# Two-layer decoder trunk: the second layer's residual and softmax sums turned by VectorE and placed through DRAM by GpSimd, and the first two blocks of a tail run in turns

## The chip, the cores and the metric

One core of a Trainium2 chip runs the whole program. The metric is device time in microseconds (us) of one execution, as the median of several runs. The engines are called as in the profile: PE is TensorE's matmul, PEld its weight load, DVE is VectorE, ACT is ScalarE, POOL is GpSimd, and SP is the engine that issues the transfers (DMAs) of the kernel before.

## The reference

The input has 1024 tokens of width 1024. Two layers follow each other; everything is float32.

```python
# layer 0: gated linear attention, layer 1: sparse attention with an indexer
y = gla_mixer(x, ...)   # then   y = dsa_mixer(x, ...)
x = layer_norm(ALPHA * x + y, ln_g[i], ln_b[i])                 # ALPHA = 4 ** 0.25
x = x + (p[i] @ ple_w[i]) * jax.nn.sigmoid(x @ ple_gate_w[i])   # the tail of a layer
# dsa_mixer, for each block of 128 queries:
score = sum over 8 index heads of relu(qi @ ki) * wi            # causal
idx = top 256 keys of each query
probs = softmax(q @ k[idx] * 128 ** -0.5)                       # 16 heads of 128, one k and v for all
o = probs @ v[idx]
return (o * silu(z)) @ w_out
```

## The kernel before

Products are made in three passes: a factor is split into a high part and the rest (`whi`, `wlo` for weights; `xh`, `xl` for activations), and high x high, high x low and low x high are added in one PSUM bank. So most of PE's work is 128x128 weights against 128x512 values, three for each 128 of depth; a block of 128 outputs over depth 1024 (`fm_block`) is 24 of them.

The tokens are done in two halves of 512. Layer 0 is done for both halves, then layer 1's index scores and top-k selection are set up, then layer 1 is done for half 0 and for half 1. Within layer 1 a half is a row of *slots*, one for each of the 16 heads: in a slot PE runs two or three blocks of projections (queries `dq`, gates `dz`, outputs `do`) with the attention of one head threaded between them. A head's scores of four query tiles (`A(t)`, into `P`) are exponentiated by ACT into `sq`, turned by DVE in squares of 32 (L1559), stored to DRAM (`sqd`), and loaded back turned (`PT`); ACT and DVE split them (`ph`, L1597 and L1599) and PE multiplies by the values (`o`). The store of a head must be done before ACT may write the next head's exponentials to `sq`.

The order of each engine is written by the program itself: `Flow` keeps a clock of PE's planned time, `fl.at(t, f)` and `after(dt, f)` put a step where that clock passes t, and every engine then takes its instructions in the order in which they were written. A wait of one instruction holds all that stand behind it on that engine. SP issues all transfers of the kernel before, on one queue.

Three places matter here.

- **The residual of layer 1.** x lies in DRAM (`x2s`) with features in rows; it is needed with tokens in rows (`y`), scaled by ALPHA. In each of the first four slots of a half, `residual` loads two tiles of 128 features x 512 tokens (`xst`, L1495), PE turns each with four transposes into a PSUM bank (`by_token`, L1500), and ACT copies it to `y` (L1501). The output products (`do`) add to `y`, and their first needs all eight.
- **The softmax sums.** For each head, `inverse` takes the reciprocal of the sums (`sm`, L1605), `turn` transposes them on PE into a PSUM bank (L1611), ACT copies them (L1616), SP stores them as a `row` (L1617), and `to_all` loads them into all partitions (`inv`, L1625), for DVE to multiply into the gate (L1647).
- **The tail.** After the normalization, PE transposes y (`xpose`), ACT and DVE make the split tiles of x (`gx` and others), and eight gate blocks follow one after the other; the first walks over the eight tiles of x as they come.

In layer 0, `squares_out` and `squares_in` already bring a result to the other orientation in the way that the change uses: DVE turns squares (L731), SP stores four quarters to DRAM (`od`, L750) and loads them back (`uf`, L756).

Of the kernel before, what the change touches and what calls it, by code (L numbers as in the profile page):

```python
# [20 lines left out]
D = 1024  # L21
L = 1024
NH = 2
HT = 512
# [253 lines left out]
def trunk_kernel(ctx, tc, x_tok, x_T, p_T, pos, freq, g_q, g_k, g_v, g_z, g_a, g_a2, g_ba, g_gn, g_o,  # L278
# [178 lines left out]

    def narrow(w, n, t):
# [170 lines left out]
    def core_steps(u):  # L629
# [175 lines left out]
    def accumulate(parts, U, y, ch, rs=None, norm=None, ahead=1):  # L805
# [5 lines left out]
        for t, b in order:  # L811
# [11 lines left out]
            ys = y[:, t, ch * 512:ch * 512 + 512]  # L823
            if rs is not None:
                dve.scalar_tensor_tensor(ys, ps, rs[:, t:t + 1], ys, op0=OP.mult, op1=OP.add)
            else:
                dve.tensor_add(ys, ps, ys)  # L827
# [26 lines left out]
    def norm_steps(y, np_, eps, on_act=()):  # L854
# [6 lines left out]
        def norm(t, ch):  # L861
# [7 lines left out]
            dve.bn_stats(st8[:, t, ch], y[:, t, ch * 512:ch * 512 + 512])  # L869
# [5 lines left out]
            def apply():  # L875
                if t in on_act:
                    act.activation(y[:, t], y[:, t], AF.Identity, scale=rstd[:, t:t + 1], bias=mv[:, t, 1:2])
                else:
                    dve.tensor_scalar(y[:, t], y[:, t], mv[:, t, 0:1], rstd[:, t:t + 1],
                                      op0=OP.subtract, op1=OP.mult)  # L880
# [24 lines left out]
    def tail(layer, Pt, y, y_done, final, tp, xps, x_alloc, tmp, ple=(), first=None, shared=False, split_last=False):  # L905
# [10 lines left out]
        def xpose(k):  # L916
            fl.need(lambda: all(y_done))
            ps = xps()
            for t in range(4):
                fl.transpose(ps[:, t * 128:t * 128 + 128], y[:, t, k * 128:k * 128 + 128], ident)  # L920
# [20 lines left out]
        for b in range(NK):  # L941
            def ev(ps, ts=slice(0, HT), b=b):
# [3 lines left out]
                def gated():  # L946
# [3 lines left out]
                      (1.5, lambda: final(b, x1, ts) if cut else final(b, x1)))  # L950
            cut = split_last and b == NK - 1
            yield from fm_block(("t", layer, b), X, ev, *([(slice(0, 256), slice(256, HT))] if cut else []))
# [50 lines left out]
    def small_head(half, X, f32t, alloc, qalloc, tmp, spsum, kih, kil, res):  # L1003
# [30 lines left out]
        yield from fm_block(("ki",), X, ev_ki)  # L1034
        for b in range(4):
            def ev_qi(ps, b=b):
# [11 lines left out]
            yield from fm_block(("qi", b), X, ev_qi)  # L1048

    def small_kv(half, X, f32t, alloc, tmp, spsum, kh, kl, vh, vl, res):  # L1050
# [14 lines left out]
        def ev_v(ps):  # L1065
# [14 lines left out]
            chain((0, lambda: act.activation(vf, ps, AF.Copy, scale=0.5)), (1.2, turn))  # L1080
# [144 lines left out]
    def start_half(half):  # L1225
# [15 lines left out]
        def feed():  # L1241
            if half == 0:
                load(0, 1)
                W.loads(W.ns + 1)
                load(1, 1)
                W.loads(W.ns + 2)
                for k in range(2, NK, 2):
                    load(k, 2)
# [28 lines left out]
    for half in range(NH):  # L1277
        hs = slice(half * HT, half * HT + HT)
        if half == 0:
# [8 lines left out]
            feed_by(feeder, 0.0, 0.0)  # L1288
# [5 lines left out]
        y = X.y  # L1294

        def load_y(y=y, half=half):
# [50 lines left out]
        norm, y_done = norm_steps(y, lp, EPS / ALPHA ** 2)  # L1347
# [141 lines left out]
    def residual(st, y, half, ks, start, end):  # L1489

        tiles = {}

        def load(k):
# [399 lines left out]
```

## Time and profile before

| | |
|---|---|
| runs of the kernel before | 1946.26 us median of 3 (1946.18 to 1946.48) |
| the profiled execution | 1945.97 us, of which the span from its first to its last instruction is 1944.2 us |
| PE busy | 1924.8 us, 99% of the span |
| DVE, ACT, POOL busy | 1481.8, 1014.5 and 55.2 us |
| DMA | 480.50 MB, mean 247 GB/s, all but some instruction loads on SP's queue |

A row of the profile names line, engine, operation, the tile written and those read, partitions x elements, and then busy time, the mean of one, and the idle time before it with what ended most of it. In a timeline the columns are start, length, engine, line and operation. The recorded length of a matmul is longer than the time after which the next one starts: matmuls overlap, and what a matmul costs PE is the distance from its start to the next start. In a table of windows DMA share is the mean busy share of 16 DMA engines, which can come out a little over 1.

### The profile page before, as it was taken

How to read it: one execution, taken by the hardware profiler on the slowest of the kernel's cores; microseconds unless marked ns; L12 is line 12 of the kernel's file. 1: busy time of each engine (PE TensorE's matmuls, PEld its weight loads, DVE VectorE, ACT ScalarE, POOL GpSimd, SP SyncE). 2: the span in 40 equal slices, each digit the busy share in tenths (PEclk: the TensorE clock that was granted, in tenths of full speed). 3: DMA queues.
4: the chain of work that ended last, by engine and by line, in shares of the span. 5: the costliest groups of instructions: out<-in, count | busy, mean ns of one | idle time of the engine just before them, and what ended most of it. 6: DMA issues, size and time to landing. Idle time of an engine off the chain costs nothing.

```text
span 1944.2 us, 26708 instructions
## 1 busy us (share of the span) xinstructions
PE 1924.8 (99%) x8912; PEld 1596.4 (82%) x8912; DVE 1481.8 (76%) x3039; ACT 1014.5 (52%) x1930; POOL 55.2 (3%) x115
## 2 busy tenths in 40 slices
PE   9999999999999999999999999999999999999999
PEld 7888888888788888888888888888878888888877
DVE  5777666696778888888859987778797887777873
ACT  5564636445564646464635676766443554434432
POOL 0000000010000000000100000000000000000000
PEclk9999999999999999999999999999999999999999
DMA  4567776767668777677686588877867998888873
GB/s 155 201 222 229 221 226 214 227 210 268 227 196 266 226 212 233 220 226 218 207 304 222 194 308 292 276 271 259 317 221 236 365 323 300 299 297 300 294 260 144
DMA packets 195818, 480.50 MB, mean 247 GB/s; under 512 B 22496, under 2 KB 39008, under 8 KB 189536
## 3 DMA queue, kind: packets, MB, share of 16 engines
q1 hardware_dynamic: 195680, 478.79, 73.8%
q8 instruction: 70, 1.15, 0.2%
q14 instruction: 68, 0.56, 0.1%
HBM read 338.98 MB, written 139.72 MB: 246 GB/s over the span
## 4 chain that ended last, share of the span: by engine, by line
PE 88%; DVE 4%; ACT 4%; DMA 2%; issue 1%; SPq 0%; POOL 0%; ACTq 0%; DVEq 0%
PE pb L58 66%; PE o L58 8%; PE U L58 6%; PE S L58 6%; DMA wlo<-wls 1%; PE tr L58 1%; ACT x L926 1%; DVE wlo L191 0%; DVE bn L869 0%; DMA xst<-x2s 0%; DMA y<-in_x_T 0%; DVE y L827 0%; PE pb L62 0%; PE ix L58 0%; DMA row<-uf 0%
## 5 line engine op out<-in xcount | busy, mean ns | idle before, releaser
L58 PE MATMUL pb<-x,whi 128*128 128x512 f32 x2272 | 705.4, 391 | 1.1 <-DVE x L411 1.0
L58 PEld LDWEIGHTS pb<-x,whi 128*128 128x128 f32 x2272 | 418.2, 188 | 81.2 <-DVE x L411 2.2
L58 PE MATMUL pb<-x,wlo 128*128 128x512 f32 x1136 | 442.8, 390 | 0.0
L58 PE MATMUL pb<-whi,u 128*128 128x512 f32 x1024 | 339.9, 392 | 1.5 <-ACT u L419 0.8
L58 PEld LDWEIGHTS pb<-x,wlo 128*128 128x128 f32 x1136 | 213.2, 188 | 45.7 <-DVE wlo L191 0.4
L58 PEld LDWEIGHTS pb<-whi,u 128*128 128x128 f32 x1024 | 192.1, 188 | 41.4 <-ACT u L419 1.2
L58 PE MATMUL pb<-wlo,u 128*128 128x512 f32 x512 | 199.8, 390 | 0.5 <-DMA wlo<-wls 0.5
L191 DVE TENSOR_TENSOR wlo<-wst,whi 128x512 fp32r<-128x512 f32 x232 | 154.3, 684 | 37.5 <-ACT whi L189 37.4
L189 ACT ACTIVATE whi<-wst 128x512 fp32r<-128x512 f32 x232 | 136.5, 622 | 69.4 <-DMA wst<-in_g_k 23.5
L1553 ACT ACTIVATE sq<-P,mx 128x128 f32<-128x128 f32 (+7 forms) x128 | 98.9, 773 | 88.2 <-DVE mx L1546 67.5
L58 PE MATMUL S<-kT,q 128*128 128x512 f32 (+2 forms) x576 | 122.4, 342 | 0.0
L1599 ACT ACTIVATE ph<-PT 128x512 fp32r<-128x512 f32 (+2 forms) x160 | 86.6, 559 | 65.6 <-PE o L58 46.3
L58 PEld LDWEIGHTS S<-kT,q 128*128 128x128 f32 x576 | 100.8, 188 | 18.1 <-DVE mx L1546 0.7
L58 PEld LDWEIGHTS pb<-wlo,u 128*128 128x128 f32 x512 | 96.2, 188 | 19.3 <-DMA wlo<-wls 1.3
L1597 DVE TENSOR_TENSOR PT<-PT,ph 128x512 fp32r<-128x512 f32 (+2 forms) x160 | 93.3, 594 | 21.1 <-ACT ph L1599 20.7
L1180 ACT ACTIVATE tk<-sc,tki 128x768 f16<-128x768 f32 (+2 forms) x90 | 92.8, 1031 | 18.3 <-DVE tki L1189 16.1
L1559 DVE STREAM_TRANSPOSE sq<-sq 128x128 f32<-128x128 f32 (+7 forms) x128 | 97.6, 768 | 3.2 <-ACT sq L1553 3.0
L237 DVE TENSOR_TENSOR pst<-pst,phi 128x512 fp32r<-128x512 f32 x130 | 88.7, 683 | 7.5 <-ACT phi L233 7.4
L736 ACT ACTIVATE junk<-o 128x512 bf16<-128x512 f32 x32 | 19.1, 597 | 142.1 <-DVE ot L731 109.8
L58 PE MATMUL o<-ph,vT 128*128 128x512 f32 (+2 forms) x320 | 92.4, 370 | 0.2 <-ACT ph L1599 0.2
L58 PE MATMUL pb<-whi,x 128*128 128x512 f32 x256 | 85.2, 391 | 0.7 <-ACT whi L189 0.7
L58 PE MATMUL U<-whi,x 128*128 128x512 f32 x256 | 84.5, 389 | 0.0
(324 smaller groups left out, 3325.0 us busy)
## 6 DMA issues: line engine op xcount, KB each, us to landing
whi<-whs SPq DMA_DIRECT2D x128, 512.0 KB
wlo<-wls SPq DMA_DIRECT2D x128, 512.0 KB
sqd<-sq SPq DMA_DIRECT2D x192, 256.0 KB
PT<-sqd SPq DMA_DIRECT2D x48, 1024.0 KB
whs<-phi SPq DMA_DIRECT2D x130, 256.0 KB
wls<-pst SPq DMA_DIRECT2D x130, 256.0 KB
wst<-in_g_z SPq DMA_DIRECT2D x32, 512.0 KB
wst<-in_g_o SPq DMA_DIRECT2D x32, 512.0 KB
```

The lines of the kernel that those rows point to most:

```text
L58: self.pe.matmul(out, lhsT, rhs, start=start, stop=stop)
L189: self.nc.scalar.activation(hi[:, c], st[:, c], AF.Copy, scale=1.0 if gain is None else gain)
L191: self.nc.vector.tensor_sub(lo[:, c], st[:, c], hi[:, c].bitcast(F32))
L237: self.nc.vector.tensor_sub(st, st.bitcast(F32), hi.bitcast(F32))
L736: act.activation(junk, ps, AF.Square, accum_out=u["ss"][:, c:c + 1])
L926: act.activation(X1[k], ps, AF.Identity, scale=g, bias=b)
L1180: act.activation(junk()[:, :n], scs[j], AF.Sign, bias=cand[:, j:j + 1].bitcast(F32), accum_out=cnt[:, j:j + 1])
L1553: act.activation(to, rows, AF.Exp, scale=-1.0, bias=mx, accum_out=sm[:, t:t + 1])
L1559: dve.transpose(x, x)
L1597: dve.tensor_sub(lo, lo.bitcast(F32), hi.bitcast(F32))
L1599: chain((0, lambda: act.activation(hi, lo.bitcast(F32), AF.Copy)), (0.8, second))
```

## The change

- `residual` uses PE and ACT no more. POOL issues the load of a tile, DVE turns its squares of 32 into a second tile (`turn`), POOL stores that in four quarters to DRAM (`rd`, pieces of 512 bytes) and loads it back with tokens in rows (`yt`). The two tiles of a slot start 7 us apart, each turned 3.5 us of plan after its load. `y` is now a function that gives the view of a token tile: runs of 32 values with 128 between their starts. ALPHA is left out and goes into the value scale and the norm's eps instead.
- `inverse` sets a small tile to zero on POOL, DVE writes the reciprocals into it and turns it in place, and POOL stores four rows of 32 to DRAM. PE's transpose, ACT's copy and SP's store go. The step moves from 3 us before the slot's end to 8.5 us (half 0) and 12 us (half 1) after its start.
- The normalized rows of layer 1 go to eight tiles of 512 (`yn`), two for each token tile.
- `fm_two` takes two blocks and runs the first 4 (or 5) tiles of x for the one, then for the other, then the rest of each. It is used for the first two gate blocks of all four tails, and for `ki` with the first `qi` block.
- In layer 0, `s3` waits until 2.2 in place of 1.6 us after its input; at the start of the program x's tiles are split 1.3 us apart in place of at once, and the load of tiles 2 and 3 is issued ahead of the second weight.

```diff
+    def fm_two(keys, X, evacs, cut):
+        parts = [W.take(key) for key in keys]
+        banks = [pbank() for _ in keys]
+        for ks in (range(cut), range(cut, NK)):
+            for (hi, lo), ps, evac in zip(parts, banks, evacs):
+                for k in ks:
...
+                        mm(ps, l[:, at], r, i == 0, i == 3 * NK - 1)
...
-                fl.ripe(st["At", c] + 1.6)
+                fl.ripe(st["At", c] + 2.2)
...
+        yield from fm_two([("t", layer, b) for b in range(2)], X, [gate(b, False) for b in range(2)], 4)
+        for b in range(2, NK):
...
+        yield from fm_two([("ki",), ("qi", 0)], X, [ev_ki, query(0)], 5)
...
                 load(1, 1)
+                load(2, 2)
                 W.loads(W.ns + 2)
...
-            feed_by(feeder, 0.0, 0.0)
+            feed_by(feeder, 0.0, 1.3)
...
         def load(k):
-            tiles[k] = xp.tile([128, HT], F32, tag="xst", name="xst", bufs=2)
-            nc.sync.dma_start(tiles[k], x2s[k, :, half * HT:(half + 1) * HT])
-
-        def by_token(k):
-            ps = pbank()
-            for t in range(4):
-                fl.transpose(ps[:, t * 128:t * 128 + 128], tiles[k][:, t * 128:t * 128 + 128], ident)
-            act.activation(y[:, :, k * 128:k * 128 + 128], ps.rearrange("p (t c) -> p t c", c=128), AF.Copy,
-                           scale=ALPHA)
-            st["y"] = k + 1
+            pool.dma_start(tile(k), x2s[k, :, half * HT:(half + 1) * HT])
+
+        def turn(k):
+            t = tiles[k]
+            sq = tile(k)
+            dve.transpose(sq.rearrange("p (m b i) -> p b m i", m=4, b=4), t)
+            after(1.0, lambda: away(k))
+
+        def away(k):
+            rd = dp.tile([4, 32, 4, 128], F32, tag="rd", name="rd", bufs=4)
+            for a in range(4):
+                pool.dma_start(rd[:, :, a].rearrange("m r x -> r m x"),
+                               tiles[k][32 * a:32 * a + 32].rearrange("p (m x) -> p m x", m=4))
+
+            def back():
+                pool.dma_start(y[:, k], rd.rearrange("m r a x -> (m r) (a x)"))
+                st["y"] = st.get("y", 0) + 1
+            after(3.0, back)
 
         for i, k in enumerate(ks):
-            fl.at(start + 0.6 * i, lambda k=k: load(k))
-            fl.at(end - 3.6 + 1.6 * i, lambda k=k: by_token(k))
+            fl.at(start + 7.0 * i, lambda k=k: load(k))
+            fl.at(start + 3.5 + 7.0 * i, lambda k=k: turn(k))
...
-            dve.reciprocal(st["sm", h], st["sm", h])
-            after(1.5, turn)
...
-            fl.transpose(ps[0:4, 0:128], st["sm", h], ident)
+            sums = l1.tile([128, 32], F32, tag="bn", name="sums")
+            pool.memset(sums, 0.0)
+            dve.reciprocal(sums[:, 0:4], st["sm", h])
+            dve.transpose(sums, sums)
...
-                act.activation(inv, ps[0:4, 0:128], AF.Copy)
-                nc.sync.dma_start(row, inv)
+                for a in range(4):
+                    pool.dma_start(row[:, 32 * a:32 * a + 32], sums[32 * a:32 * a + 4])
...
-                fl.at(start + dur - 3.0, scale[0])
+                fl.at(start + (12.0 if half else 8.5), scale[0])
```

How the instructions stand, at three places.

**POOL, layer 1, half 0, second slot.** `sq` is the exponentials' tile, `rstd` and `mv` belong to the norm at the end of the half. Before, POOL has nothing between them:

```order
L1762 MEMSET sq 128x2048
L863 TENSOR_SCALAR rstd<-mv 128x1
L864 TENSOR_TENSOR rstd<-rstd,mhalf 128x1
L866 TENSOR_SCALAR mv<-mv,rstd 128x1
L863 TENSOR_SCALAR rstd<-mv 128x1
```

Now, from the slot's first tile on:

```order
L1527 DMA xst<-x2s 128x512
L1542 DMA y<-rd 128x512
L1538 DMA rd<-xst 32x4x128 x4
L1527 DMA xst<-x2s 128x512
L1647 MEMSET sums 128x32
L1542 DMA y<-rd 128x512
L1654 DMA row<-sums 4x32 x4
L1538 DMA rd<-xst 32x4x128 x4
```

In half 0 the memset that DVE's reciprocal waits for stands behind four stores and one load of the same slot. (In half 1 it stands one further back, behind `y<-rd` as well.)

**DVE, layer 1, half 0, third slot.** `q` is a query tile's low part, `z` the gate, `PT` the low part of the exponentials, `tk`, `tki` and `tkf` the top-k selection. Before:

```order
L1186 TENSOR_TENSOR tki<-tkf 128x4
L1187 SCALAR_TENSOR_TENSOR tki<-tki 128x4
L1189 TENSOR_SCALAR tki<-tki 128x4
L1559 STREAM_TRANSPOSE sq<-sq 128x4x3x32
L411 TENSOR_TENSOR q<-qf,q 128x512
L1559 STREAM_TRANSPOSE sq<-sq 128x16x32
L1462 SCALAR_TENSOR_TENSOR z<-z,pb 128x512
L1597 TENSOR_TENSOR PT<-PT,ph 128x4x128
L1136 TENSOR_SCALAR tk,tkf<-sc_9850,tki 128x640
L1597 TENSOR_TENSOR PT<-PT,ph 128x4x96
L1605 RECIPROCAL sm<-sm 128x4
```

After:

```order
L1532 STREAM_TRANSPOSE xst<-xst 128x4x4x32
L1163 TENSOR_SCALAR tk,tkf<-sc_9850,tki 128x640
L1600 STREAM_TRANSPOSE sq<-sq 128x4x3x32
L1213 TENSOR_TENSOR tki<-tkf 128x4
L1214 SCALAR_TENSOR_TENSOR tki<-tki 128x4
L1216 TENSOR_SCALAR tki<-tki 128x4
L411 TENSOR_TENSOR q<-qf,q 128x512
L1600 STREAM_TRANSPOSE sq<-sq 128x16x32
L1491 SCALAR_TENSOR_TENSOR z<-z,pb 128x512
L1648 RECIPROCAL sums<-sm 128x4
L1649 STREAM_TRANSPOSE sums<-sums 128x32
L1638 TENSOR_TENSOR PT<-PT,ph 128x4x128
```

The turn of the slot's first tile has come in, and the reciprocal, eight instructions after it, stands ahead of the split of `PT` in place of behind two thirds of it.

**PE, the tail of layer 1, half 0**, from the fourth tile of x in the first gate block. `gx`, `z` and `rt` are the split tiles of x in their order, z the first. Before, the second gate block begins at the last row:

```order
L58 MATMUL pb<-gx,whi 128x512 x2
L58 MATMUL pb<-gx,wlo 128x512
L58 MATMUL pb<-gx,whi 128x512 x2
L58 MATMUL pb<-gx,wlo 128x512
L58 MATMUL pb<-gx,whi 128x512 x2
L58 MATMUL pb<-gx,wlo 128x512
L58 MATMUL pb<-gx,whi 128x512 x2
L58 MATMUL pb<-gx,wlo 128x512
L58 MATMUL pb<-gx,whi 128x512 x2
L58 MATMUL pb<-gx,wlo 128x512
L58 MATMUL pb<-z,whi 128x512 x2
```

After:

```order
L58 MATMUL pb<-gx,whi 128x512 x2
L58 MATMUL pb<-gx,wlo 128x512
L58 MATMUL pb<-z,whi 128x512 x2
L58 MATMUL pb<-z,wlo 128x512
L58 MATMUL pb<-z,whi 128x512
L58 MATMUL pb<-rt,whi 128x512
L58 MATMUL pb<-z,wlo 128x512
```

The second block's first four tiles now stand between the first block's fourth and fifth tile.

More of the change, by code (lines that the diff above doesn't have):

```diff
@@ L875, in apply @@
             def apply():
[L876 to L880, printed above, removed]
+                for there, row in to(t):
+                    if t in on_act:
+                        act.activation(there, row, AF.Identity, scale=rstd[:, t:t + 1], bias=mv[:, t, 1:2])
+                    else:
+                        dve.tensor_scalar(there, row, mv[:, t, 0:1], rstd[:, t:t + 1],
+                                          op0=OP.subtract, op1=OP.mult)
                 f_done[t] = True
@@ L940, in tail, with gate, ev @@
             yield
-        for b in range(NK):
-            def ev(ps, ts=slice(0, HT), b=b):
+        def gate(b, cut):
+            def ev(ps, ts=slice(0, HT)):
                 sg = tmp()[:, ts]
@@ L950, in ev @@
                       (1.5, lambda: final(b, x1, ts) if cut else final(b, x1)))
+            return ev
+        yield from fm_two([("t", layer, b) for b in range(2)], X, [gate(b, False) for b in range(2)], 4)
+        for b in range(2, NK):
             cut = split_last and b == NK - 1
-            yield from fm_block(("t", layer, b), X, ev, *([(slice(0, 256), slice(256, HT))] if cut else []))
+            yield from fm_block(("t", layer, b), X, gate(b, cut),
+                                *([(slice(0, 256), slice(256, HT))] if cut else []))
     def rope_tables():
@@ L1032, in weights, with query, ev_qi @@
             res["w"] = wt
-        yield from fm_block(("ki",), X, ev_ki)
-        for b in range(4):
-            def ev_qi(ps, b=b):
+        def query(b):
+            def ev_qi(ps):
                 qf = f32t()
@@ L1047, in ev_qi @@
                 rope(qf, ci, si, swap_i, tmp, stack)
-            yield from fm_block(("qi", b), X, ev_qi)
+            return ev_qi
+        yield from fm_two([("ki",), ("qi", 0)], X, [ev_ki, query(0)], 5)
+        for b in range(1, 4):
+            yield from fm_block(("qi", b), X, query(b))
     def small_kv(half, X, f32t, alloc, tmp, spsum, kh, kl, vh, vl, res):
@@ L1245, in feed @@
                 load(1, 1)
+                load(2, 2)
                 W.loads(W.ns + 2)
-                for k in range(2, NK, 2):
-                    load(k, 2)
+                load(4, 2)
+                load(6, 2)
                 nc.sync.dma_start(ba, g_ba)
@@ L1293, in trunk_kernel, with y, load_y @@
             X, units, feeder, _ = nxt
-        y = X.y
-        def load_y(y=y, half=half):
+        def y(t, a, n, tile=X.y):
+            return tile[:, t, a:a + n]
+        def load_y(y=X.y, half=half):
             nc.sync.dma_start(y, x_tok[half * HT:(half + 1) * HT, :].rearrange("(t p) d -> p t d", p=128))
```

47 lines of the change are left out of this document (32 added, 15 removed).

## The prediction

> **What bounds the kernel.** I read the page first, then the groups and waits of PE, then its timeline where it stops, then a table of windows for the slots of layer 1 that hold the residual.
>
> ```profile
> span 1944.2 us, 26708 instructions
> PE 1924.8 (99%) x8912; PEld 1596.4 (82%) x8912; DVE 1481.8 (76%) x3039; ACT 1014.5 (52%) x1930; POOL 55.2 (3%) x115
> PE 88%; DVE 4%; ACT 4%; DMA 2%; issue 1%; SPq 0%; POOL 0%; ACTq 0%; DVEq 0%
> ```
>
> PE is the bound from end to end: 99% busy, and 88% of the chain that ended last. An instruction taken off PE is therefore worth its distance to the next start, as long as nothing that PE needs comes later. The profiled execution took 1945.97 us (1.8 us around the span), 0.3 under the median of 1946.26; sums below are made against 1945.97.
>
> ```profile
> 1130.00:1147.00 17.00, 16.82 (x87) 13.75 (x86) 13.82 (x38) 14.60 (x34) 0.00 (x0) 1.00 0.85 300
> 1147.00:1164.00 17.00, 16.01 (x82) 13.30 (x81) 14.16 (x40) 14.11 (x34) 0.00 (x0) 1.00 0.83 288
> 1516.00:1537.00 21.00, 21.00 (x106) 17.68 (x105) 19.24 (x41) 11.42 (x23) 0.00 (x0) 1.00 0.99 361
> 1537.00:1558.00 21.00, 21.00 (x105) 17.65 (x105) 18.08 (x38) 11.43 (x23) 0.00 (x0) 1.00 0.97 344
> 1550.00:1555.00 5.00, 5.00 (x24) 4.14 (x23) 5.00 (x8) 2.67 (x5) 0.00 (x0) 1.00 1.01 406
> ACT sq L1553 <- DMA sqd<-sq: 13.2, 4, 4.0
> ```
>
> The columns are the window, then us busy of PE, PEld, DVE, ACT and POOL, PE's clock, DMA share and GB/s. Two slots of half 0 (17 us each), two of half 1 (21 us), and a short stretch. In half 1 the DMA engines are 97 to 99% busy and DVE 86 to 92%: two resources lie close behind PE, just where the change puts more on both. The last row, from ACT's waits between 1495 and 1600 us, says that ACT already waits there for the store of the exponentials, in four slots up to 4.0 us.
>
> **What comes off PE.**
>
> ```profile
> L62 PE MATMUL pb<-ident,xst 128*128 128x128 f32 x64 | 9.6, 273 | 1.0 <-DMA xst<-x2s 1.0
> L62 PE MATMUL S<-ident,sm 128*4 128x128 f32 x32 | 8.7, 271 | 0.0
> 1113.92 0.39 PE L58 MATMUL pb<-x,wlo 128*128 128x512 f32 x1
> 1114.15 0.60 PE L62 MATMUL pb<-ident,xst 128*128 128x128 f32 x4
> 1114.50 0.72 PE L58 MATMUL o<-ph,vT 128*128 128x512 f32 x2
> 1115.06 0.39 PE L58 MATMUL o<-PT,vT 128*128 128x512 f32 x1
> ...
> 1165.80 0.34 PE L58 MATMUL o<-PT,vT 128*128 128x384 f32 x1
> 1165.97 0.27 PE L62 MATMUL S<-ident,sm 128*4 128x128 f32 x1
> 1166.00 0.71 PE L58 MATMUL pb<-x,whi 128*128 128x512 f32 x2
> 1166.54 0.40 PE L58 MATMUL pb<-x,wlo 128*128 128x512 f32 x1
> ```
>
> A matmul of 512 columns costs 0.23 us (1113.92 to 1114.15). Residual: from 1114.15 to 1115.06 stand four transposes and two matmuls, 0.91 us; without the transposes 0.46; so 0.45 for a tile, and 64/4 = 16 tiles give 7.2 us. Sums: from 1165.80 to 1166.54 is 0.74 us; a 384-column matmul (0.17, 1165.80 to 1165.97) and two of 512 make 0.63; so 0.11, and 32 of them 3.5 us. The wait for `xst` goes as well: 1.0 idle and the restart after it, say 1.2 us. All three certain as far as PE's list goes: 11.9 us.
>
> **Stops that other edits aim at.**
>
> ```profile
> 12.44 0.39 PE L58 MATMUL pb<-whi,x 128*128 128x512 f32 x1
> 13.07 0.50 PE L58 MATMUL pb<-wlo,x 128*128 128x512 f32 x1 [0.24 <-DVE wlo L191]
> ...
> 14.88 0.50 PE L58 MATMUL pb<-wlo,x 128*128 128x512 f32 x1 [0.84 <-DVE wlo L191]
> 15.21 0.63 PE L58 MATMUL pb<-whi,x 128*128 128x512 f32 x2
> 893.45 0.39 PE L58 MATMUL o<-v,Ah 128*128 128x512 f32 x1
> 894.53 0.50 PE L58 MATMUL o<-v,Al 128*128 128x512 f32 x1 [0.69 <-DVE Al L411]
> 1420.71 0.62 PE L58 MATMUL pb<-gx,whi 128*128 128x512 f32 x2
> 1426.31 0.62 PE L58 MATMUL pb<-z,whi 128*128 128x512 f32 x2
> ```
>
> Start: 12.44 to 15.21 is 2.77 us for five starts, worth 1.14; DVE was splitting x ahead of the second weight's low part. Spread 1.3 us apart, x leaves room for it; I take 1.5, bounds 0 and 1.6 (the weight's load moves behind 512 KB and could be late itself). `s3`: 0.85 lost at 894, and the added 0.6 us holds one group of three matmuls in between, 0.6; bounds 0 and 0.85. Pair of gate blocks: from the fourth tile of x (1420.71) to the next block (1426.31) are 15 starts, 3.4 us; it took 5.6, so 2.2 lost to tiles not yet split. The second block's four tiles give the fifth 12 x 0.23 = 2.7 us more time: I take 2.0, bounds 0 and 2.2. The other pairs (three tails and `ki`) show no such loss, nothing. ACT's two halves of a normalized row cost what the whole did, and the tail's PE has other work then: nothing. Together 4.1 us.
>
> Gains: 11.9 + 4.1 = 16.0 us.
>
> **What it loads elsewhere.**
>
> ```profile
> L731 DVE STREAM_TRANSPOSE ot<-o 128x512 f32<-128x512 f32 x29 | 20.8, 716 | 22.4 <-PE o L58 22.2
> L1559 DVE STREAM_TRANSPOSE sq<-sq 128x128 f32<-128x128 f32 x16 | 4.8, 300 | 0.0
> L1559 DVE STREAM_TRANSPOSE sq<-sq 128x384 f32<-128x384 f32 x16 | 8.9, 556 | 0.2 <-ACT sq L1553 0.2
> L1136 DVE TENSOR_SCALAR_CACHE_REDUCE tk<-sc,tki 128x640 f16<-128x640 f32 x31 | 26.8, 863 | 1.5 <-ACT tk L1180 1.5
> L411 DVE TENSOR_TENSOR q<-qf,q 128x512 fp32r<-128x512 f32 x32 | 21.6, 676 | 0.8 <-ACT q L419 0.8
> L1189 DVE TENSOR_SCALAR tki<-tki 128x4 int32<-128x4 int32 x30 | 5.1, 170 | 1.0
> L750 SPq DMA_DIRECT2D od<-ot x116: 303/434/1762, 87.2 to 917.9; - x116
> ```
>
> DVE: two turns of 512 columns in a residual slot (0.716 each, L731 of layer 0 does the same) and one small turn (at most the 0.300 of 128 columns) make 1.73 us. Half 0: 14.16 + 1.73 = 15.9 of 17. Half 1: 19.24 + 1.73 = 20.97 of 21 in the fullest slot, 19.8 in the next. It fits with next to no room; 0.5 us for the fullest slot, bounds 0 and 1.7 x 8 = 14. In the later slots (24 sums of 0.3) it is hidden, DVE not being full there. ACT loses 16 copies and 32 small ones; it was not the bound.
>
> POOL: no trace of before shows a transfer issued by POOL. SP's issue of the same quarter stores took 0.43 us in the median and 1.76 at most; in the middle, 1.1 us each. In half 0 the memset of the sums stands behind five issues of the slot, which start when DVE has turned the first tile. DVE's own eight instructions from that turn to the reciprocal take 0.86 + 0.56 + 3 x 0.17 + 0.68 + 0.7 + 0.68, about 4.0 us. So DVE stops for 5 x 1.1 - 4.0 = 1.5 us, of which 17 - 15.9 = 1.1 us was free: 0.4 in each of four slots, 1.6 us. Bounds: nothing at 0.43; (8.8 - 5.1) x 4 = 15 us at 1.76. Behind DVE's reciprocal then wait the low parts of `PT` and the multiplication by `inv`, and for them PE's products with the values. In half 1 there are seven issues' worth ahead of it but 7.5 us of plan and the four large turns of the exponentials between: nothing, bounds 0 and 15 again.
>
> The Trainium skill, on its page "SBUF — State Buffer", section "Who interferes with whom", says that a DVE instruction in a two-port mode (copies and `tensor_scalar` without an accumulator are named) shuts GpSimd out for its whole length, descriptors for its DMAs included. By that rule the issues would wait; but the eight instructions of the slot are turns, two-input ones, accumulating counts and one small `tensor_scalar` of 0.17 us, so it would add about 0.2 us a slot and the sum stays as it is. No run so far shows a POOL transfer to hold against it.
>
> DMA: a tile's load is not new. New are its store in pieces of 512 bytes and its load back, 2 x 0.26 MB, so 1.05 MB in a slot. Half 1: 344 GB/s x 21 us = 7.2 MB become 8.3. At the 406 GB/s of the short stretch they need 20.3 us, less than the slot; at 344/0.97 = 355 GB/s, 23.3 us, or 2.3 over. Bounds 0 and 4 x 2.3 = 9.2 us. The loads run at the faster rate, the stores at the slower; I take 1.0 us a slot, 4 us: the store of the exponentials lands later, ACT's wait for it (4.0) grows, and behind it PE's next head. In half 0 288 GB/s x 17 us + 1.05 MB = 5.9 MB need 17 us at 288/0.83 = 347 GB/s: just full, nothing, bounds 0 and 2.
>
> Given back: 0.5 + 1.6 + 4.0, and 0.4 for restarts: 6.5 us. Sum: 1945.97 - 16.0 + 6.5 = 1936.5 us.
>
> **Rivals.**
> *Everything new is hidden*: POOL issues at SP's median, transfers fill holes, DVE's turns fall in its gaps. For it speaks that PE hardly stopped (19 us of 1944) with DVE that full; against it, ACT's wait for the stores. 1945.97 - 16.0 = 1930.
> *The DMA engines are the bound of half 1's four slots*, and half 0's too: 9.2 + 2 us, and DVE's fullest slots one more: 1945.97 - 16.0 + 12.2 = 1942 to 1945, within 0.2% or at its edge. For it speaks the share of 0.97 to 0.99; against it, that 406 GB/s were reached.
> *POOL's queue holds DVE* (the other side): at 1.76 us an issue half 0 gives back 15 us, and in half 1 seven issues and a landing, 12.3 + 3, against some 11 us of DVE work and gaps, 4 x 4 = 17: 1945.97 - 16.0 + 15 + 17 = 1962. It decides from about 1.5 us an issue, where both halves together give back the 16 us. The memset's place ahead of the reciprocal speaks for it, that POOL has nothing else to do against it.
>
> The Trainium skill's page "DMA: Bandwidth & Descriptors", section "Latency and other measured facts", gives GpSimd's path about 1 us to the first byte, against 0.6 for the other engines'; an estimate by that figure, were it the cost of an issue, would be 1.0 for my 1.1, 2 us less in the sum.
>
> **How the numbers follow.** My forecast (some given back, 1931.5 to 1941) 0.50, all hidden 0.20, DMA bound (1941 to 1950) 0.20, POOL holds DVE 0.10. Within 0.2%, about what can be told from no change, is 1942.4 to 1950.2: the slower part of the DMA case, 0.16; faster 0.50 + 0.20 + 0.04 = 0.74; slower 0.10. The range reaches from 1929 (all hidden, all bounds of the gains) to 1948, into the DMA case, and leaves out the POOL case and the rest, less than 0.2.
>
> **What would show it.** PE's groups without `xst` and `sm`; no idle time at 13 to 15 us and in the pair of gate blocks; POOL's issues near 1.1 us; in half 1's slots DMA share at 1.0, ACT's wait for `sqd` longer than 4.0 us and PE idle for `PT` or `ph`; slots of half 0 that stay at 17 us less the transposes. Wrong would be an idle DVE ahead of the reciprocal with POOL as its releaser over 2 us in each slot, or slots of half 1 longer than 22 us.

## The result, and the profile after

The changed kernel took 1974.39 us (1972.43 to 1975.87, 4 runs) against 1946.37 us for the kernel before: a ratio of 1.0143, 95% interval 1.0125 to 1.0161, 28 us slower. The forecast was 1936.5 us in a range of 1929 to 1948. Of the cases only one, to which 0.10 was given, lay on the slow side; even that was put at 1962, and its mechanism isn't the one found below.

From the page: the span, the busy times, and the chain that ended last.

```profile
span 1974.1 us, 26929 instructions
PE 1929.0 (98%) x8816; PEld 1599.9 (81%) x8816; DVE 1497.9 (76%) x3091; ACT 1000.5 (51%) x1886; POOL 178.5 (9%) x371
PE 83%; DMA 8%; DVE 4%; issue 2%; ACT 2%; POOL 1%; SPq 0%; DVEq 0%; ACTq 0%; POOLq 0%
```

PE has 96 matmuls fewer and yet is busy 4.2 us longer. DMA has gone from 2% of the chain to 8%.

Where the time went is read from four starts of PE: the first transpose of the tail in half 0 and in half 1, two of the kernel before and two of the changed one (timelines).

```profile
1412.35 1.03 PE L62 MATMUL S<-ident,y 128*128 128x128 f32 x8
1890.83 1.03 PE L62 MATMUL S<-ident,y 128*128 128x128 f32 x8
```

```profile
1422.34 1.03 PE L62 MATMUL S<-ident,yn 128*128 128x128 f32 x8
1920.54 1.03 PE L62 MATMUL S<-ident,yn 128*128 128x128 f32 x8
```

"Half 1" below is the distance between the two, 478.5 us before and 498.2 after; "half 0" is the distance from the last product of the index scores (1096.98 and 1093.68 us) to the first of them, 315.4 and 328.7. What comes ahead is 3.3 us shorter, and what comes behind the same (53.4 and 53.6). So the whole loss lies in layer 1's two halves, and there in the eight slots that hold the residual. PE's score products (`S<-kT,q`) of before and after, compared one by one, show it: ahead of these slots in half 0 they come 3.3 us earlier than before and behind them 11.8 us later, in half 1 7.7 and 31.9 us later, and in the other slots the distance shrinks a little. The same windows as in the prediction, or next to them, in the same columns:

```profile
1114.00:1131.00 17.00, 13.71 (x54) 11.38 (x53) 10.37 (x25) 4.40 (x11) 5.65 (x11) 0.80 0.84 298
1131.00:1148.00 17.00, 13.99 (x61) 11.32 (x60) 13.43 (x37) 11.16 (x25) 8.41 (x16) 0.90 0.86 269
1516.00:1537.00 21.00, 17.90 (x78) 14.54 (x77) 15.98 (x36) 7.55 (x15) 6.10 (x12) 0.92 1.00 367
1537.00:1558.00 21.00, 16.92 (x67) 13.43 (x66) 14.60 (x27) 7.24 (x13) 7.77 (x15) 0.84 0.73 234
```

PE stops for 3 to 4 us in each, DVE is *less* busy than before, not fuller, and PE's granted clock is 0.80 to 0.92 where it was 1.00. DVE's waits, the first two rows for 1097 to 1190 us, the third for 1505 to 1640 us, say why it is less busy (waits in all, how many, the longest):

```profile
DVE xst L1532 <- DMA xst<-x2s: 7.6, 3, 3.4
DVE xst L1532 <- issue: 3.4, 3, 2.2
DVE xst L1532 <- issue: 17.8, 5, 5.9
```

DVE stands 28.8 us in all before the turn of a residual tile (L1532), and everything behind the turn stands with it. (In the rows with "issue" the profile names no releaser. By the landings in the trace it is the load: in each of the 11 waits the turn starts 0.08 to 0.45 us after its tile's load has landed, and the stores of the tile before had landed at least 1.5 us earlier.) POOL's timeline over one slot:

```profile
1128.86 0.56 POOL L1542 DMA_DIRECT2D y<-rd  x1 [8.57 <-DMA rd<-xst]
1131.08 2.33 POOL L1538 DMA_DIRECT2D rd<-xst  x4 [1.66 <-DVE xst L1532]
1133.40 0.56 POOL L1527 DMA_DIRECT2D xst<-x2s  x1
1133.95 0.14 POOL L1647 MEMSET sums<- 128x32 f32 x1
1135.23 0.55 POOL L1542 DMA_DIRECT2D y<-rd  x1 [1.14 <-DMA rd<-xst]
1135.78 2.07 POOL L1654 DMA_DIRECT2D row<-sums  x4
1139.34 1.68 POOL L1538 DMA_DIRECT2D rd<-xst  x3 [1.49 <-DVE xst L1532]
1142.10 0.55 POOL L1538 DMA_DIRECT2D rd<-xst  x1 [1.09 <-DMA y<-rd]
1142.64 0.56 POOL L1527 DMA_DIRECT2D xst<-x2s  x1
```

An issue takes 0.56 us, half of what was assumed. What takes time is the standing still: POOL waits 8.57 us at a load back for its stores to land, and at 1142 us a fourth store waits for the load back before it, which went out eight transfers earlier: the program's POOL transfers take turns on eight semaphores, and the store needs the one that the load back still holds. The load behind it, that of the next slot's first tile, goes out at 1142.64. From issue to landing, in the median, these transfers take (1097 to 1650 us):

```profile
rd<-xst POOLq DMA_DIRECT2D x64, 64.0 KB, 4.8
y<-rd POOLq DMA_DIRECT2D x16, 256.0 KB, 5.8
xst<-x2s POOLq DMA_DIRECT2D x15, 256.0 KB, 6.5
```

The plan turns a tile 3.5 us after its load. An estimate by the fit of the Trainium skill's page "DMA: Bandwidth & Descriptors", section "Anatomy of one DMA — SWDGE (gpsimd) path" (2.0 us and the bytes at 436 GB/s), would be 2.6 us for 256 KB; the trace, with the DMA engines 73 to 100% busy, has 6.5.

### The profile page after: what moved, and what is told of

It reads as the page before. It is cut to its first block, busy times and chain, and to the rows that moved or that the text cites. A ratio compares the mean times of both kernels' runs of the same rounds, so it can differ in the third digit from the quotient of the medians.

```text
span 1974.1 us, 26929 instructions
## 1 busy us (share of the span) xinstructions
PE 1929.0 (98%) x8816; PEld 1599.9 (81%) x8816; DVE 1497.9 (76%) x3091; ACT 1000.5 (51%) x1886; POOL 178.5 (9%) x371
## 4 chain that ended last, share of the span: by engine, by line
PE 83%; DMA 8%; DVE 4%; issue 2%; ACT 2%; POOL 1%; SPq 0%; DVEq 0%; ACTq 0%; POOLq 0%
PE pb L58 63%; PE o L58 7%; PE U L58 6%; PE S L58 5%; DMA xst<-x2s 2%; DMA y<-rd 2%; DMA rd<-xst 1%; POOL rd L1538 1%; DMA PT<-sqd 1%; PE tr L58 1%; DMA sqd<-sq 1%; DMA wls<-pst 0%; DVE sq L1600 0%; DVE PT L1638 0%; DVE xst L1532 0%
## 5 line engine op out<-in xcount | busy, mean ns | idle before, releaser
L58 PEld LDWEIGHTS pb<-x,whi 128*128 128x128 f32 x2272 | 423.7, 190 | 80.3 <-DVE x L411 1.8
L1654 POOL DMA_DIRECT2D row<-sums x128 | 66.3, 524 | 438.9 <-DVE sums L1649 420.2
L58 PE MATMUL o<-PT,vT 128*128 128x512 f32 (+3 forms) x224 | 74.8, 357 | 25.7 <-DVE PT L1638 25.4
```

The costliest lines, as they stand in the source:

```text
L58: self.pe.matmul(out, lhsT, rhs, start=start, stop=stop)
L1654: pool.dma_start(row[:, 32 * a:32 * a + 32], sums[32 * a:32 * a + 4])
```

## The experiments

All runs in one table. The difference is to the kernel before in the same series of runs (its medians there were 1943.9 to 1946.4); halves and clock are of the profiled run. Each kernel is described below.

| kernel | median, us | to before | ratio, 95% interval | half 0 | half 1 | PE's clock |
|---|---|---|---|---|---|---|
| before | | | | 315.4 | 478.5 | 1.000 |
| changed | 1974.39 | +28.0 | 1.0125 to 1.0161 | 328.7 | 498.2 | 0.992 |
| load on SP | 1993.71 | +48.8 | 1.0236 to 1.0266 | 340.3 | 506.5 | 0.988 |
| old residual | 1937.99 | -6.9 | 0.9952 to 0.9978 | 314.8 | 474.6 | 1.000 |
| old sums | 1974.82 | +29.9 | 1.0137 to 1.0170 | 331.0 | 494.6 | 0.993 |
| neither | 1937.66 | -7.3 | 0.9952 to 0.9978 | 313.7 | 473.8 | 1.000 |
| turn at 6.0 | 1978.14 | +33.6 | 1.0156 to 1.0186 | 335.5 | 493.6 | 0.991 |
| lead | 1966.07 | +21.6 | 1.0090 to 1.0124 | 326.7 | 489.6 | 0.993 |
| lead, loads on SP | 1969.89 | +25.4 | 1.0114 to 1.0144 | 328.3 | 491.1 | 0.993 |
| lead, zero once | 1962.65 | +18.8 | 1.0079 to 1.0115 | 326.8 | 485.9 | 0.996 |
| the same, back later | 1965.43 | +20.3 | 1.0085 to 1.0116 | 328.6 | 489.6 | 0.996 |
| own place | 1957.83 | +13.5 | 1.0053 to 1.0080 | 321.8 | 486.1 | 1.000 |
| own place, rows on SP | 1957.83 | +13.1 | 1.0054 to 1.0085 | 320.1 | 489.1 | 0.996 |
| the same in half 0 alone | 1945.70 | +1.0 | 1.0001 to 1.0019 | 320.2 | 475.5 | 0.998 |
| idle traffic, two slots | 1949.32 | +4.8 | 1.0020 to 1.0039 | 318.0 | 481.0 | 0.997 |
| there and back, three slots | 1953.72 | +9.8 | 1.0035 to 1.0067 | 323.3 | 481.2 | 0.998 |
| turns alone | 1940.45 | -3.4 | 0.9972 to 0.9992 | 314.7 | 475.8 | 0.999 |
| pieces of 2 KB | 1952.91 | +9.0 | 1.0029 to 1.0062 | 324.4 | 480.8 | 0.998 |
| there and back, zero once | 1952.60 | +7.5 | 1.0024 to 1.0051 | 324.4 | 479.8 | 0.997 |
| old residual, zero once | 1938.69 | -6.4 | 0.9955 to 0.9980 | 315.0 | 474.7 | 1.000 |

### Which part of the change

*Load on SP.* Theory: a circle of landings on POOL's queue.

```diff
-            pool.dma_start(tile(k), x2s[k, :, half * HT:(half + 1) * HT])
+            nc.sync.dma_start(tile(k), x2s[k, :, half * HT:(half + 1) * HT])
```

> The changed kernel with one word altered: the load of a residual tile is issued by SP again, the stores, the load back and the sums' rows stay with POOL. Theory (a circle on POOL's in-order queue: load back, fourth store, next load, DVE's turn, stores, load back, each waiting for the landing before; it takes 19 to 22 us in slots planned for 17 and some 27 in slots planned for 21): without the load in it the circle is open, DVE no longer stands before a turn, and the eight slots come back to 17 and 21 us: 1930 to 1940 us. Rival, the DMA engines (share 0.84 to 1.0 in these slots): the same bytes move, so not under 1965 us. Rival, the sums' place on POOL: memset and rows are where they were, so 1965 us or more.

It took 1993.71 us: 20 us worse. The theory in that form fell; both rivals had said 1965 us or more. DVE's waits between 1097 and 1200 us and between 1505 and 1640 us:

```profile
DVE xst L1532 <- DMA xst<-x2s: 22.5, 4, 7.0
DVE xst L1532 <- DMA xst<-x2s: 27.1, 4, 8.2
```

On SP's queue a load goes out behind what SP has to issue first (in half 0 the second load of a slot right behind the 1 MB of a head's exponentials), and DVE stands before the turn longer still. The gate is the turn, on either queue; which queue sets how long.

*Old residual; old sums; neither.* The parts put back as they were, each alone and both, with ALPHA left out as in the change:

```diff
-            pool.dma_start(tile(k), x2s[k, :, half * HT:(half + 1) * HT])
+            nc.sync.dma_start(tiles[k], x2s[k, :, half * HT:(half + 1) * HT])
...
-            dve.transpose(sq.rearrange("p (m b i) -> p b m i", m=4, b=4), t)
+                fl.transpose(ps[:, t * 128:t * 128 + 128], tiles[k][:, t * 128:t * 128 + 128], ident)
```

```diff
-            pool.memset(sums, 0.0)
-            dve.reciprocal(sums[:, 0:4], st["sm", h])
-            dve.transpose(sums, sums)
+            dve.reciprocal(st["sm", h], st["sm", h])
+            after(1.5, turn)
...
+            fl.transpose(ps[0:4, 0:128], st["sm", h], ident)
```

> The changed kernel with the residual as it was (SP's load, PE's four transposes, ACT's copy), the sums still on DVE and POOL. Theory of the circle: it is gone, PE has 7.2 us of transposes and some 1.2 us of waits for xst back: 1930 + 8.4 = 1938 us. Rival of the DMA engines: 1 MB a slot less, 1938 too. Rival of the sums: 1965 us or more, since memset, reciprocal and rows remain.

> The changed kernel with the sums as they were (PE's transpose, ACT's copy, SP's row), the residual still on DVE and POOL. Theory of the circle: four issues of 0.52 us leave it, and the load back waits for fewer landings, but load, turn and store still follow each other: PE has its 3.5 us back, the slots lose 4 to 5 us in place of 5 to 6: 1955 to 1972 us. Rival of the sums: the loss is gone, 1930 + 3.5 = 1934 us. Rival of the DMA engines: as the changed kernel, with 3.5 us more: 1975 us or so.

> The changed kernel with both residual and sums as they were: what is left are the blocks in turns, the later s3, the start, ALPHA in the scales and the norm's rows in tiles of 512. Every theory: the predicted 4.1 us of these, 1942 us; 1944 or more would mean that the stops only moved.

The residual is the whole loss: without it 1937.99, without the sums 1974.82. The sums' move is worth nothing either way (1937.99 with it, 1937.66 without), although it takes 32 transposes off PE. And what is left of the change without both beats both kernels: 7.3 us under the kernel before, more than the 4.1 forecast for it.

### Which wait

*Turn at 6.0* and *lead*: the turn 2.5 us of plan later; or each load issued right after the turn of the tile before, some 8 us ahead of its own turn, on POOL or on SP.

```diff
-            fl.at(start + 3.5 + 7.0 * i, lambda k=k: turn(k))
+            fl.at(start + 6.0 + 7.0 * i, lambda k=k: turn(k))
```

```diff
             dve.transpose(sq.rearrange("p (m b i) -> p b m i", m=4, b=4), t)
+            if k + 1 < NK:
+                load(k + 1)
...
-            fl.at(start + 7.0 * i, lambda k=k: load(k))
-            fl.at(start + 3.5 + 7.0 * i, lambda k=k: turn(k))
+            fl.at(start + (5.0 + 9.5 * i if half else 4.0 + 8.0 * i), lambda k=k: turn(k))
```

> The changed kernel with one number altered: a tile is turned 6.0 us of plan after its load is put, not 3.5. Theory (after the load's move to SP made it slower: whichever queue issues it, the load takes 4.7 us and up to 9.9 to land, or 5.5 to 6.5 behind SP's stores of the exponentials; the plan gives it 3.5; DVE stands at the turn for the rest, and all that is behind it on DVE with it): 2.5 us more for each of 16 tiles take away most waits of the median landing, not those of the long ones: 1938 to 1955 us. Rival, the 1 MB a slot on the DMA engines and the turns on DVE cost the time by themselves, wherever they stand: no gain, 1970 us or more.

> The changed kernel with each load issued right after the turn of the tile before, ahead of that tile's stores on POOL's queue, and the turns 8.0 us apart in half 0, 9.5 and the rest of the slot in half 1; the same transfers, the same turns. Theory of the short lead: with some 8 us between load and turn DVE finds the tile there; the 46 us of stops in the eight slots go down to a few: 1930 to 1940 us. Rival of the bytes and turns: 1965 us or more. Rival of POOL's queue (at most eight of its transfers seem to be under way at a time, so that the fourth store waits for a load back): the loads are still late behind it, 1945 to 1965 us.

> As the run with the loads moved ahead, and the loads issued by SP in place of POOL. Theory of the short lead: the same 1930 to 1940 us, as the queue makes no difference once the lead is long. Rival of POOL's queue: clearly under the run with POOL's loads, by 5 us or more. Rival of bytes and turns: 1965 us or more.

The theory of the load's lead alone missed in all three. With the turn at 6.0 it took 1978.14 us, with the lead 1966.07 and, on SP, 1969.89, each on the side of the rival that bytes and turns cost the time. DVE's waits say what happened; with the turn at 6.0 in half 0 (first two rows) and in half 1:

```profile
DVE sums L1648 <- POOL sums L1647: 5.5, 3, 2.3
DVE xst L1532 <- DMA rd<-xst: 5.0, 3, 2.5
DVE sums L1648 <- POOL sums L1647: 11.2, 4, 4.9
```

The waits for the load are gone (2.1 us are left), and two others stand in their place: the reciprocal waits for POOL's memset, which is queued behind a load back, and the turn waits for the stores of the tile before to leave the second of only two tiles. One gate for another, and no gain. With the lead the memset's is 9.2 us in half 1.

*Lead, zero once* and *back later*. The sums get two tiles of their own, set to zero once; then the load back is issued 7 us after the stores in place of 3.

```diff
-            sums = l1.tile([128, 32], F32, tag="bn", name="sums")
-            pool.memset(sums, 0.0)
+            sums = two_sums[h % 2]
```

```diff
-            after(3.0, back)
+            after(7.0, back)
```

> The run with the loads moved ahead on POOL (1966.1 us), and the sums kept in two tiles of their own that POOL sets to zero once, so that the reciprocal on DVE no longer waits for a memset behind a load back on POOL's queue. Theory (two causes: DVE stands at gates that POOL opens late, and the new transfers slow the others): DVE's 9.2 us of waits for the memset in half 1 go, half 1 of layer 1 shrinks by 5 to 9 us, half 0 stays: 1957 to 1961 us. Rival of one gate taking the place of another (as it did when the turn was put later): DVE stands elsewhere, 1964 us or more. Rival that transfers are all: no change.

> The run with loads moved ahead and tiles set to zero once (1962.7 us), with the load back issued 7 us of plan after the stores in place of 3. Theory (in half 0 DVE waits 9.2 us for the stores of the tile before, out of the second of two tiles; POOL issues these late since it stands 35 us at loads back whose stores haven't landed): POOL's waits at the load back shrink to under half and DVE's with them; half 0 from 326.8 to some 320 us, half 1 as it is or 2 us less: 1954 to 1959 us. Rival, the stores' own landing holds the tile: no change, 1961 us or more.

The first gave 1962.65 us, 1.7 above the range: the gain is all in half 1, as expected, but 3.7 us in place of 5 to 9. The second missed: 1965.43. POOL's waits at loads back in half 0 fell from 35 to 7 us, yet DVE's wait for the second tile stayed (9.2 us in half 0 in the first run, 9.1 in the second), so it is the stores' own landing that holds the tile, not POOL's place in its queue.

*Own place.* Each tile is turned into the place in y to which it comes back in the end; the two tiles are then for loads alone.

```diff
-            sq = tile(k)
+            sq = y[:, k]
...
-            if k + 1 < NK:
-                load(k + 1)
+            if k + 2 < NK:
+                load(k + 2)
```

> The run with loads moved ahead and tiles set to zero once (1962.7 us), with each tile turned into the place that it will have in y in the end, so that the two tiles are for loads alone and each load goes out a whole turn earlier; same transfers, same turns. Theory (gates and transfers are the whole): no turn waits any more; what is left are the transfers. Half 0: the old residual's 315.0 less 3.6 us of transposes plus some 4 us of transfers, 315 us in place of 326.8; half 1: 474.7 less 3.6 plus 7, 478 us in place of 485.9; with 1094.2, 53.5 and 1.7 around them 1940 to 1947 us. Rival, the gate was only where the time showed and the transfers' own price is most of it: half 0 stays over 322 us, 1955 us or more.

1957.83 us, above the range of 1940 to 1947; half 0 came down by 5.0 to 321.8, half 1 not at all. The rows of its waits, DVE and SP in half 0, ACT in half 1 (1490 to 1610 us):

```profile
DVE y L1532 <- DMA xst<-x2s: 0.8, 1, 0.8
SPq L1664 <- DMA row<-sums: 26.0, 8, 8.4
ACT sq L1597 <- DMA sqd<-sq: 29.0, 4, 9.9
```

Only one turn still waits, 0.8 us. But the rows of the sums stand on POOL's queue behind the loads back, SP waits for them at its load of `inv`, and the weights stand behind that.

*Rows on SP*, and then the residual on PE in half 1:

```diff
-                    pool.dma_start(row[:, 32 * a:32 * a + 32], sums[32 * a:32 * a + 4])
+                    nc.sync.dma_start(row[:, 32 * a:32 * a + 32], sums[32 * a:32 * a + 4])
```

> The run that turns each tile into its own place (1957.8 us), with the four rows of the sums issued by SP in place of POOL. Theory (in half 0 the queue of POOL holds SP, and SP the weights; in half 1 the transfers themselves): half 0 from 321.8 to 314 to 317 us; half 1 stays within 3 us of 486: 1950 to 1954 us. Rival, the transfers cost both halves: half 0 stays over 320, 1956 us or more.

> The same in half 0 and the old residual (PE's transposes) in half 1; the sums on DVE in both, rows issued by SP. Theory (half 0 has room for the transfers, half 1 had none): half 0 314 to 317 us, half 1 474 to 476 us, in all 1937 to 1941 us. Rival, transfers cost both halves: half 0 over 320, 1944 us or more.

1957.83 and 1945.70 us. SP's wait was not the rest: it went from 26.0 to 2.1 us, but half 0 stayed at 320, the rival's side of both expectations. In half 1 the 13.6 us between the two runs are what the residual costs there net of its eight groups of transposes.

### What the transfers cost by themselves

These stand on the old residual with the new sums (1937.99 us), with the new residual's work beside it on data that nobody needs: first with a second load of each tile, in two slots of each half; then only what the change adds, in three slots; then turns without transfers, and stores in pieces of 2 KB. The turn has a tile of its own (`to`), the stores take another (`x`), the load back goes to a third.

```diff
+        def turn(k):
+            dve.transpose(to, to)
+            after(1.0, lambda: away(k))
...
+            for a in range(4):
+                pool.dma_start(rd[:, :, a].rearrange("m r x -> r m x"),
+                               x[32 * a:32 * a + 32].rearrange("p (m x) -> p m x", m=4))
+            after(3.0, lambda: pool.dma_start(spare[1], rd.rearrange("m r a x -> (m r) (a x)")))
```

> The kernel with the old residual and the new sums (1938.0 us), and beside it, in the first two slots of each half, the new residual's load, turn, four stores and load back for two tiles a slot on the same engines and queue, with data that nobody needs and no wait between them: load, turn and store each work on a tile of their own. Theory of the short lead: the traffic and the turns cost little by themselves, 1938 to 1943 us. Rival of bytes and turns: half of the eight slots lose what they lose in the changed kernel, about half of 36 us: 1955 us.

> The kernel with the old residual and the new sums (1938.0 us), and beside it in three of the four slots of each half only what the change adds: two turns on DVE, two times four stores in pieces of 512 bytes and two loads back, on data that nobody needs and with no wait between them. (The run with traffic had a second load of each tile as well, and two slots a half; it took 11.3 us more, 3.3 in half 0 and 6.4 in half 1 by the two profiles.) Theory of two causes: two thirds of those bytes in three slots for two, as much again: 1946 to 1951 us. Rival, the added loads made that cost: 1940 us or less. Rival that transfers and turns are all of the change's loss: 1938 + 3/4 of 44, 1971 us.

> The same without its transfers: only the two turns on DVE a slot, in three slots of each half. Theory of two causes: DVE has room for 1.4 us a slot, 1938 to 1940 us. Rival, DVE is the full engine and the transfers cost nothing: as the run with turns and transfers.

> As the run with turns and transfers in three slots, with the stores in pieces of 2 KB in place of 512 bytes; the same bytes. If the small pieces make the price: 3 us or more under that run, towards 1940 us. If the bytes do: the same within 2 us.

> The run with turns, stores and loads back in three slots of each half beside the old residual (1953.7 us), with the sums' tiles set to zero once. Now neither DVE nor PE nor ACT stands behind anything that POOL does, but for the sums' rows. Theory (in half 0 the price of that run, 8.6 us, was DVE at the memset, which POOL reached late, 7.3 us of DVE's waits there; in half 1, where DVE did not wait for it, the 6.6 us are the transfers': ACT waits for the stores of the exponentials): half 0 comes back to within 3 us of the old residual's 314.8, half 1 stays near 481: 1943 to 1948 us. Rival, the transfers cost both halves alike: 1951 us or more. Rival, all was the queue: 1940 us or less.

> The kernel with the old residual and the new sums, tiles set to zero once, so that DVE's reciprocal doesn't wait for POOL, nor POOL's memset for the landing of the rows before. If the memset was what took back the sums' 3.5 us of PE: 1934 to 1936 us, the fastest of all. If it was something else (the rows land 5 us after POOL's issue, the transposes' place next to xst's wait): 1938 us as before, no better than the kernel with both as they were.

The idle traffic in two slots took 1949.32 us, between its two expectations; turns and transfers in three slots 1953.72, 2.7 above the range. Differences to before compared, the turns alone cost 3.5 us, 1.2 of it in half 1 and none in half 0 by the profiles. Turns and transfers cost 16.7 us in three of four slots, and the size of the pieces makes no difference (1953.72 and 1952.91). Zeroing once took 1 to 2 us off that (1952.60, on the rival's side: I had put all of half 0's share down to the memset), and nothing off the old residual (1938.69). How the transfers cost is seen in half 1, where no engine waits for the idle traffic itself. ACT's wait for the stores of the exponentials (1490 to 1610 us), and those stores' landing (last column, 1495 to 1560 us), first of the old residual with tiles set to zero once:

```profile
ACT sq L1582 <- DMA sqd<-sq: 13.5, 4, 4.4
```

```profile
sqd<-sq SPq DMA_DIRECT2D x24, 256.0 KB, 5.9
```

Then with the transfers beside it:

```profile
ACT sq L1598 <- DMA sqd<-sq: 25.3, 5, 6.1
```

```profile
sqd<-sq SPq DMA_DIRECT2D x22, 256.0 KB, 7.6
```

The stores land 1.7 us later and ACT waits 12 us more (6.5 more than in the run of the old residual without zeroing once, which has 18.8). Its wait for the load back of the exponentials (`PT`) grows as well, from 3.3 to 14.2 us. In three windows of 21 us from 1497 us on, the DMA engines move 337, 349 and 366 GB/s, against 372, 346 and 345 without the extra bytes, at shares of 0.95 to 1.01 in both: they were full, so the new bytes push back the others. That POOL's packets take their turns with SP's fits the Trainium skill's page "DMA: Bandwidth & Descriptors", section "SWDGE vs HWDGE vs iDMA" (each path feeds a queue of its own in a DMA engine, which goes round them); no run here takes the queues apart.

Half 0's share of that run, 9.4 us, is partly its own: PE's old transposes wait for their load, which the changed kernel doesn't have.

```profile
1168.39 1.08 PE L62 MATMUL pb<-ident,xst 128*128 128x128 f32 x4 [4.87 <-DMA xst<-x2s]
```

## Why the prediction was wrong

By its own steps:

*What comes off PE* (11.9 us): the transposes are gone from the list, yet those of the sums, 3.5 us, moved no clock (1937.99 against 1937.66). In the slots without a residual PE does gain by them, 0.12 us a slot in half 0 and 0.07 in half 1 (0.11 was priced). It gives most of this back before the residual's old transposes in half 0, two stops of the run with the old residual and the new sums:

```profile
1128.77 0.63 PE L62 MATMUL pb<-ident,xst 128*128 128x128 f32 x4 [1.67 <-ACT tk L1207]
1161.51 0.63 PE L62 MATMUL pb<-ident,xst 128*128 128x128 f32 x4 [1.38 <-DMA xst<-x2s]
```

These waits make 3.1 us there and 3.4 with tiles set to zero once, so the memset isn't their cause; with both parts old the wait at this place is 0.2. Why they grow stays open. The residual's 7.2 can't be seen under what it brought.

*Stops* (4.1 us): right in kind and low in size: 7.3 us measured with neither part, 4.3 to 9.3 by the interval. By the two profiles, which lie 9.4 us apart, 3.1 of it stand ahead of layer 1's heads, where 2.1 were forecast, and 2.3 in the tail of half 0, where 2.0 were forecast; 3.4 stand at the ends of the two halves, behind the last scores and ahead of the tails, for which nothing was forecast.

*DVE* (0.5 us, bounds 0 to 14): low but in its bounds; turns alone cost 1.2 to 3.5 in three of four slots.

*POOL* (1.6 us at 1.1 us an issue): the step that failed first. I priced the issue and took it for what a queue costs. The groups of POOL, mean of one in ns in the third column:

```profile
L1654 POOL DMA_DIRECT2D row<-sums x128 | 66.3, 524 | 438.9 <-DVE sums L1649 420.2 <-DVE tki L1214 16.8 <-issue 1.8
L1538 POOL DMA_DIRECT2D rd<-xst x64 | 35.7, 562 | 95.9 <-DVE xst L1532 75.0 <-DVE sums L1649 13.0 <-DMA y<-rd 3.9
L1542 POOL DMA_DIRECT2D y<-rd x16 | 8.9, 558 | 54.1 <-DMA rd<-xst 41.3 <-issue 10.4 <-ACT qf L1480 2.4
```

An issue is 0.52 to 0.56 us, near my lower bound, where I wrote "nothing". But POOL stood 41.3 us at loads back for the stores to land, and the loads behind them went out late. "A tile's load is not new" is the step that put the largest cost at nothing: the bytes weren't new, the lead was. Before, PE used the tile 12 us of plan and more after its load; now DVE does, 3.5 us after, and a landing takes 6.5, so that DVE stood 28.8 us before the turns. Of the two signs of being wrong that the prediction named, the slots of half 1 came (23.9 to 28.2 us from one head's first scores to the next one's, against 22); DVE was not idle ahead of the reciprocal, since it stood at the turn. The rival "POOL's queue holds DVE" had the side and the place, not the mechanism, and its point of decision, 1.5 us an issue, was wrong: it happened at 0.56.

*DMA* (4 us in half 1, none in half 0): mis-sized. Once no engine stands at a gate of POOL's queue (own place, rows on SP), half 0 is 8.9 us and half 1 18.1 above what the old residual less its 3.6 us of transposes a half gives (311.2 and 471.0): 27 us, of which the runs with idle traffic account for some 12 (below). I had compared bytes with what the engines can move in a slot. In half 1 what counts is when a store lands, since ACT's next exponentials wait for it. For half 0, where the share was 0.83 to 0.93 before, the runs don't show that: with the tiles in their own place ACT waits 1.8 us for these stores (1097 to 1200 us), and they land after 5.0 us in the median, against 7.5 with the old residual (1097 to 1165 us). What lands later there is the load back of `PT`, 7.6 us against 5.1, and PE's stops end with ACT's and DVE's work on `q` (3.1 us), `PT` (2.8) and `ph` (2.0).

*Restarts* (0.4 us): mis-sized too. PE in the changed kernel, and at the same place in the run with tiles turned into their own place:

```profile
1119.22 1.23 PE L58 MATMUL S<-kT,q 128*128 128x256 f32 x4 [3.29 <-DVE q L411]
1120.24 1.05 PE L58 MATMUL pb<-x,whi 128*128 128x512 f32 x2
1121.10 0.63 PE L58 MATMUL pb<-x,wlo 128*128 128x512 f32 x1
...
1125.67 0.40 PE L58 MATMUL pb<-x,wlo 128*128 128x512 f32 x1
1125.90 0.62 PE L58 MATMUL pb<-x,whi 128*128 128x512 f32 x2
```

```profile
1119.88 0.74 PE L58 MATMUL S<-kT,q 128*128 128x256 f32 x4 [3.06 <-DVE q L411]
1120.45 0.62 PE L58 MATMUL pb<-x,whi 128*128 128x512 f32 x2
1120.91 0.39 PE L58 MATMUL pb<-x,wlo 128*128 128x512 f32 x1
```

After a stop of 3.29 us two matmuls of 512 columns take 0.86 us (1120.24 to 1121.10) in place of 0.46, and so it goes on to 1125.67. Counted over the trace, 47 matmuls of 512 columns start 0.40 to 0.46 us ahead of a next one that waits for nothing, and none do in the kernel before. Over the usual 0.23 they cost 9.4 us: so much of the loss are stops paid a second time by the clock.

The account, as far as the runs go. From the changed kernel (28.0 us above before) to the one with no gate at a turn (13.5) are 14.5 us: gates and their restarts. From there to the old residual (-6.9) less its 7.2 us of transposes are 27.6 us. Turns and transfers beside the old residual gave 13.9 us in three of four slots, 4.9 of them that run's own; the rest, by four thirds, is 12, an estimate. So some 15 of the 27.6 us, the larger part of them in half 1, aren't explained by any single run: they show in ACT's waits for stores (29.0 us in a window of half 1, where 13.5 to 18.8 are usual) and in DVE's order, and remain open. A third tile, which would have tested the two-tile gate more plainly, wasn't tried.

## What to carry to other kernels

A transfer that is moved onto another queue is priced first by its lead, from its issue to its first use, against the landing time under the load of that stage, and only then by its issue and its bytes; where the plan gives 3.5 us and landings take 3 to 10, an in-order engine stands at the use with all its other work. When a gate is opened and the time stays, read the engines' waits again: here the load, the memset and the second tile held DVE in turn, and the rows held SP at no price that shows. And 7 us of PE's work moved onto DMA engines that were 83 to 99% busy cost more than they had on PE; the best version found (1937.66 us, ratio 0.9952 to 0.9978, and no different with the sums moved) leaves both residual and sums where they were and keeps the blocks in turns, the later `s3`, the start, the scales and the norm's rows in tiles of 512.

## What the runs showed of the hardware

PE's clock, not only its idle time, pays for a stop. In the changed kernel's trace the granted clock is 0.50 in seven stretches of 3.4 or 6.8 us, all in the residual's slots, as in this one (columns of the tables of windows):

```profile
1118.60:1125.40 6.80, 6.18 (x17) 5.29 (x18) 3.76 (x12) 2.95 (x8) 1.10 (x2) 0.50 0.97 354
```

Stops of 2.54 to 4.08 us were followed by 3 to 10 matmuls at 0.43 us in place of 0.23, and three shorter stops close together, the longest of 1.76 us, by six. At one and the same place a stop of 3.06 us (own place) was followed by none and one of 3.05 us (own place, rows on SP) by five, so the length of the stop alone doesn't decide. The Trainium skill's page "TensorE: Matmul & The Clock Gate", section "Part 1: The HAM clock gate (the "warmup" mystery)", says that an idle window of about 3.4 us halves PE's clock until about as long a stretch of work has passed; the trace agrees on the half and on the length, and shows it after shorter stops too.

A row of 0.5 KB issued by POOL landed after 3.9 us in the median, hardly sooner than 64 KB (4.8). At most eight of POOL's transfers were under way at a time, which is the number of semaphores that this program gives them in turn and isn't shown to be a limit of the chip: the fourth store stood for the load back eight before it (1.09 us at 1142.10).
